# Second parts of split weights issued right behind the first parts in a two-layer streaming encoder

## The chip, the cores and the metric

The kernel runs on one core of a Trainium2 chip. The metric is the device time of one execution in microseconds (us). The kernel before took 1279.29 us, the median of three runs (1280.31, 1279.29 and 1275.89).

The core's engines each work through their own instructions in the order in which the program lists them, and wait for each other by semaphores: PE (TensorE) multiplies matrices, with its weight loads shown as PEld; DVE (VectorE) and ACT (ScalarE) work elementwise; POOL (GpSimd) does little here; SP (SyncE) issues the DMA transfers.

## The reference

A trunk of two layers over 256 frames with 1024 channels, in float32. Each layer has a token mixer and a channel mixer, both modulated by a conditioning vector (shift, scale, gate):

```python
# token mixer: an RG-LRU group (512 channels) beside differential attention (4 heads)
h  = rmsnorm(x) * (1 + scale) + shift
z  = h @ w_in                      # 1024 x 2560: lru input, gelu gate, q, k, v
a  = exp(-8 * sigmoid(conv(z) @ wa + ba) * softplus(-lam))
y0 = scan(a, sqrt(1 - a*a) * (i * conv(z))) * gelu(z_gate)
y1 = rmsnorm((softmax(q0 k0) - lambda * softmax(q1 k1)) @ v)   # rope on q, k; chunk mask
x  = x + gate * (concat(y0, y1) @ w_out)
# channel mixer: layer 0 dense, layer 1 top 2 of 8 experts
x  = x + gate * ((silu(h @ wg) * (h @ wu)) @ wd)               # inner width 3072
```

The weights are some 420 MB of float32, read once from HBM.

## The kernel before

**Splitting.** Every product is to be as exact as float32, and is built from three matmuls over numbers of a shorter format: with w = wh + wl and x = xh + xl it sums xh·wh, xh·wl and xl·wh (`mm3`, L203 to L213; in the token mixer's input projection the same three are written out: `proj_T`, L568 to L583, and `queries_keys`, L585 to L597, where L593 holds the two products with wh and L596 the one with wl). For the activations `cut` makes the parts (`hh`, L565, and `hl`, L566). Weights arrive by DMA as `raw` tiles of 128 x 2048 (10 buffers) and are split in pieces of 128 x 1024 by `split_next` (L137): ACT copies the piece into the short format, the first part `wh` (L147); DVE subtracts it from the raw piece, the second part `wl` (L148). Both have 4 buffers. Not all weights are split: those of the modulation (`adaps`, L404) and of most expert units are multiplied as they are.

**The order.** It is written by hand: each engine runs its instructions as the Python code records them. The unit of this order is the quarter chunk, one piece of weights. `quarter` (L159) first runs the `tick`: all elementwise or small PE work that was put off to this quarter by `after` (constants at the start, rotary embedding, softmax, the gates and the scan of the LRU, silu, and so on). Then `refill` (L169) splits pieces until 4 are ready, and `piece` (L164) hands one of them to the matmuls. The second part of a piece is not recorded with the first: `split_next(False)` puts it as a function into `self.rests`, and `split_rest` (L154) records the oldest one:

```python
nc.scalar.activation(wh, raw, AF.Copy)                                               # L147
self.rests.append(lambda: nc.vector.tensor_tensor(wl, raw, wh.bitcast(F32), op=ALU.subtract))  # L148
self.ready.append((wh, wl))
if whole:
    self.split_rest()
```

`refill` counts the second parts that were pending when it began (`old`), splits the first parts of new pieces, and then records `old` second parts. So the wl of a piece is recorded one `refill` after its wh, with the tick between them standing ahead of it in DVE's order; `piece` makes up for it when the piece that it hands out would still lack its wl.

**The stages, by the trace.** Layer 0: token mixer to about 155 us, dense SwiGLU to 365 us. Layer 1: token mixer 370 to 485 us, routing to 508 us, then eight expert units (`glu_unit`, three of them on all 256 frames, with split weights: from 508, 690 and 790 us; the others partly or wholly on unsplit weights). In the mixers, `adaps`, `hps` (L541), `colps` (L415) and the gain (L417) make the modulated input of one quarter of the channels, and `zps` are queries and keys; `vps` are the values and `wops` the output projection (L208 to L210). In a big expert unit `mul` (L858, DVE) multiplies silu by the up projection and `flip` (L863, PE) transposes the result two quarters later.

Of the kernel before, what the change touches and what calls it, by code (L numbers as in the profile page):

```python
# [74 lines left out]
class Kernel:  # L75
# [86 lines left out]
        return self.piece(n)  # L162

    def piece(self, n):  # L164
        if len(self.rests) >= len(self.ready):
            self.split_rest()
        return [w.rearrange("p (a b) -> p a b", a=n) for w in self.ready.pop(0)]

    def refill(self, most=1 + AHEAD):  # L169

        old = len(self.rests)
        while len(self.ready) < most and self.spos < self.limit and self.split_at(self.spos * PIECE // RAW):
            self.split_next(False)
        for _ in range(old):
            self.split_rest()

    def warm(self, n):

# [1746 lines left out]
```

## Time and profile before

| | before |
|---|---|
| median of 3 runs | 1279.29 us (1275.89 to 1280.31) |
| profiled execution, its span | 1276.7 us, 1274.8 us |
| PE busy | 1223.6 us, 96% |
| DVE busy | 687.7 us, 54%; wl (L148) 344 times, 408.2 us |
| ACT busy | 554.2 us, 43%; wh (L147) 344 times, 359.7 us |
| mean granted TensorE clock | 0.986 of 2.4 GHz |

The profile is of one execution. A row of its timeline gives start and duration in us, engine, line, operation, output<-input, and in brackets how long the engine had been idle before and what ended the idle time. Busy shares are averages over stages: an engine that is 96% busy over the whole can still wait at a few places, and those places are what a change of order can reach.

### The profile page before, as it was taken

To read this page: it belongs to the slowest core of one execution; us is meant where nothing else is said; L and a number is where in the kernel's file an instruction comes from. 1 tells how busy PE (TensorE), PEld (TensorE's weight loads), DVE (VectorE), ACT (ScalarE), POOL (GpSimd) and SP (SyncE) were. 2 spreads that over 40 slices of the span, in tenths; PEclk is the share of its full clock that TensorE was granted. 3 is DMA by queue.
4 is the path that set the end of the run, shared out by engine and by line. 5 is a ranking of instruction groups with operands and counts; after the bars stand their busy time and mean duration, and the time that the engine had idled before them with its cause. 6 is when DMAs were issued, how large, how long until landed. Compare 5 with 4: busy or idle time off the path is not lost.

```text
span 1274.8 us, 19410 instructions
## 1 busy us (share of the span) xinstructions
PE 1223.6 (96%) x7702; PEld 813.0 (64%) x7702; DVE 687.7 (54%) x992; ACT 554.2 (43%) x809; POOL 21.3 (2%) x40
## 2 busy tenths in 40 slices
PE   5899999999999989999998999999999999999995
PEld 4777799999978768788434888888433333333332
DVE  4677687776567766988404889999401001100102
ACT  3466454444444945888203888788210000010001
POOL 1000100000000000000000000000000000000001
PEclk9999999999999988999999999999999999999998
DMA  9976788887544346899999999999999999998994
GB/s 374 418 304 229 275 315 300 308 298 293 191 183 168 131 171 256 300 338 343 364 418 419 419 418 419 391 363 366 343 419 418 418 419 417 364 375 348 418 418 194
DMA packets 63427, 424.68 MB, mean 333 GB/s; under 512 B 7734, under 2 KB 7990, under 8 KB 15072
## 3 DMA queue, kind: packets, MB, share of 16 engines
q1 hardware_dynamic: 63072, 423.28, 84.5%
q8 instruction: 62, 1.02, 0.3%
q14 instruction: 37, 0.30, 0.1%
q0 software_dynamic: 256, 0.09, 0.0%
HBM read 422.29 MB, written 1.05 MB: 332 GB/s over the span
## 4 chain that ended last, share of the span: by engine, by line
PE 81%; DMA 7%; DVE 6%; ACT 4%; issue 1%; SPq 0%; POOL 0%; POOLq 0%; DVEq 0%; ACTq 0%
PE gps L889 4%; PE ups L889 4%; PE gps L580 4%; PE gps L582 4%; PE gps L578 4%; PE gps L942 3%; PE yps L981 3%; PE ups L942 3%; PE bps L954 3%; DMA raw<-i_md 3%; DMA raw<-i_mu 3%; PE ups L209 2%; PE yps L209 2%; PE ups L208 2%; PE yps L210 2%; PE ups L210 2%
## 5 line engine op out<-in xcount | busy, mean ns | idle before, releaser
L148 DVE TENSOR_TENSOR wl<-raw,wh 128x1024 fp32r<-128x1024 f32 x344 | 408.2, 1220 | 57.6 <-ACT wh L147 55.3
L147 ACT ACTIVATE wh<-raw 128x1024 fp32r<-128x1024 f32 x344 | 359.7, 1060 | 168.0 <-PE gps L580 55.9
L580 PE MATMUL gps<-hl,wh 128*128 128x256 f32 x384 | 96.5, 284 | 0.7 <-DVE hl L566 0.7
L578 PE MATMUL gps<-hh,wh 128*128 128x256 f32 x384 | 96.7, 284 | 0.1
L580 PEld LDWEIGHTS gps<-hl,wh 128*128 128x128 f32 x384 | 72.8, 190 | 1.3 <-DVE hl L566 1.1
L578 PEld LDWEIGHTS gps<-hh,wh 128*128 128x128 f32 x384 | 72.8, 190 | 0.5 <-DVE hh L565 0.3
L900 DVE TENSOR_TENSOR sgs<-sgs,ups 128x512 f32<-128x512 f32 x9 | 6.2, 688 | 120.6 <-PE ups L889 120.6
L911 PE MATMUL yps<-raw,hTs 128*64 128x512 f32 x288 | 66.9, 596 | 2.3 <-DMA raw<-i_md 2.1
L947 DVE TENSOR_TENSOR sgm<-sgm,ups 128x512 f32<-128x512 f32 x6 | 4.1, 688 | 116.6 <-PE ups L942 116.6
L889 PE MATMUL ups<-raw,ef 128*64 128x512 f32 x288 | 65.3, 594 | 0.8 <-DMA raw<-i_mu 0.8
L889 PE MATMUL gps<-raw,ef 128*64 128x512 f32 x288 | 66.0, 598 | 0.0
L582 PE MATMUL gps<-hh,wl 128*128 128x256 f32 x384 | 61.7, 283 | 0.0
L209 PE MATMUL gps<-wl,eh 128*128 128x512 f32 x144 | 57.0, 396 | 1.5 <-DVE wl L148 1.5
L208 PE MATMUL gps<-wh,eh 128*128 128x512 f32 x144 | 57.0, 396 | 1.2 <-ACT wh L147 1.2
L208 PE MATMUL yps<-wh,fh 128*128 128x512 f32 x144 | 58.0, 402 | 0.0
L209 PE MATMUL ups<-wl,eh 128*128 128x512 f32 x144 | 56.9, 395 | 0.5 <-DVE wl L148 0.5
L209 PE MATMUL yps<-wl,fh 128*128 128x512 f32 x144 | 56.7, 394 | 0.4 <-DVE wl L148 0.3
L208 PE MATMUL ups<-wh,eh 128*128 128x512 f32 x144 | 56.9, 395 | 0.0
L210 PE MATMUL gps<-wh,el 128*128 128x512 f32 x144 | 56.4, 391 | 0.0
L210 PE MATMUL yps<-wh,fl 128*128 128x512 f32 x144 | 56.3, 391 | 0.0
L210 PE MATMUL ups<-wh,el 128*128 128x512 f32 x144 | 56.3, 391 | 0.0
L582 PEld LDWEIGHTS gps<-hh,wl 128*128 128x128 f32 x384 | 52.8, 190 | 0.0
(329 smaller groups left out, 2038.8 us busy)
## 6 DMA issues: line engine op xcount, KB each, us to landing
raw<-i_mu SPq DMA_DIRECT2D x92, 1024.0 KB, 10.5
raw<-i_md SPq DMA_DIRECT2D x88, 1024.0 KB, 11.8
raw<-i_mg SPq DMA_DIRECT2D x84, 1024.0 KB, 9.5
raw<-i_ada SPq DMA_DIRECT2D x48, 1024.0 KB, 7.5
raw<-i_win SPq DMA_DIRECT2D x20, 1024.0 KB, 9.2
raw<-i_fg SPq DMA_DIRECT2D x12, 1024.0 KB, 6.8
raw<-i_fu SPq DMA_DIRECT2D x12, 1024.0 KB, 6.9
raw<-i_fd SPq DMA_DIRECT2D x12, 1024.0 KB, 6.5
```

The source lines that it names most:

```text
L147: nc.scalar.activation(wh, raw, AF.Copy)
L148: self.rests.append(lambda: nc.vector.tensor_tensor(wl, raw, wh.bitcast(F32), op=ALU.subtract))
L208: mm(out, lhsT=xh, rhs=wh, start=start, stop=False)
L209: mm(out, lhsT=xh, rhs=wl, start=False, stop=False)
L210: mm(out, lhsT=xl, rhs=wh, start=False, stop=stop)
L578: self.nc.tensor.matmul(out, lhsT=w, rhs=hh[:, k, :], stop=False, start=k == 0 and (len(ks) == NK or m + j == 0))
L580: self.nc.tensor.matmul(out, lhsT=w, rhs=hl[:, k, :], start=False, stop=False)
L582: self.nc.tensor.matmul(out, lhsT=wl[:, j * len(ks) + i, :], rhs=hh[:, k, :], start=False, stop=k == NK - 1 and (len(ks) == NK or m + j == 1))
L889: nc.tensor.matmul(ps[c * HALF:(c + 1) * HALF, :], lhsT=eh[:, k, :], rhs=w[c][i // 2][:, i % 2, :], start=k == 0, stop=k == NK - 1)
L911: self.nc.tensor.matmul(y[n * HALF:(n + 1) * HALF, :], lhsT=hT[:, b, c * HALF:(c + 1) * HALF], rhs=w[n][b // 2][:, b % 2, :], start=i == 0 ...
L942: nc.tensor.matmul(ps[q(2 * c + s), :], lhsT=eh[:, k, q(s)], rhs=ws[w][c][i // 2][:, i % 2, :], start=k == 0, stop=k == NK - 1)
L954: nc.tensor.matmul(bp[q(2 * w + c), :], lhsT=eh[:, k, q(2)], rhs=ws[w][c][i // 2][:, i % 2, :], start=k == 0, stop=k == NK - 1)
```

## The change

`refill` records the second part of every piece directly behind its first part, and no longer carries any over; `piece` no longer needs to force one.

```diff
     def piece(self, n):
-        if len(self.rests) >= len(self.ready):
-            self.split_rest()
         return [w.rearrange("p (a b) -> p a b", a=n) for w in self.ready.pop(0)]
 
     def refill(self, most=1 + AHEAD):
-
-        old = len(self.rests)
         while len(self.ready) < most and self.spos < self.limit and self.split_at(self.spos * PIECE // RAW):
-            self.split_next(False)
-        for _ in range(old):
-            self.split_rest()
+            self.split_next()
```

Instructions are neither added nor removed. The orders of PE, ACT, POOL and SP stay as they were, each DMA issue among them. On DVE the wl rows move ahead of the ticks: of some 916 other DVE rows 382 have one wl more ahead of them than before, 28 at the start have two more, and 506 have as many as before. The new file is six lines shorter, so that a line behind L175 has a number lower by 6 there.

DVE at the start of layer 0, where the constants of the rotary embedding are computed (`set_91`); before:

```order
L566 TENSOR_TENSOR hl<-hf,hh 128x256
L260 CAST set_91<-set_91 128x2
L262 TENSOR_SCALAR set_91<-set_91 128x32 x2
...
L276 TENSOR_SCALAR set_91<-set_91 128x64
L277 TENSOR_SCALAR set_91<-set_91 128x64
L148 TENSOR_TENSOR wl<-raw,wh 128x1024 x2
L408 TENSOR_TENSOR row_130<-adaps,row_130 128x128
```

and now:

```order
L560 TENSOR_TENSOR hl<-hf,hh 128x256
L148 TENSOR_TENSOR wl<-raw,wh 128x1024 x2
L254 CAST set_91<-set_91 128x2
L256 TENSOR_SCALAR set_91<-set_91 128x32 x2
...
L270 TENSOR_SCALAR set_91<-set_91 128x64
L271 TENSOR_SCALAR set_91<-set_91 128x64
L402 TENSOR_TENSOR row_130<-adaps,row_130 128x128
```

Two wl, of pieces 2 and 3 (counted from 0), moved from behind the 18 instructions of sine and cosine to ahead of them. Some 20 rows further on the wl of pieces 4 and 5 moved in the same way ahead of the differential attention's lambda (L292 to L309).

DVE in layer 0 ahead of the output projection (`gate0`: the scan's output, cut into hh and hl); the tile numbers tell which piece a wl belongs to. Before:

```order
L763 RECIPROCAL rsum_1081<-sums_1059 128x2
L148 TENSOR_TENSOR wl_1065<-raw_1015,wh_1064 128x1024
L710 TENSOR_TENSOR gate1_914<-gate1_914,th_982 128x1024
L712 SCALAR_TENSOR_TENSOR gate0_865<-a0_983,gate1_914 128x256 x4
L726 TENSOR_TENSOR gate0_865<-gate0_865,gy_1116 128x512
L565 CAST hh_1132<-gate0_865 128x512
```

and now:

```order
L757 RECIPROCAL rsum_1082<-sums_1060 128x2
L148 TENSOR_TENSOR wl_1096<-raw_1093,wh_1095 128x1024
L704 TENSOR_TENSOR gate1_915<-gate1_915,th_983 128x1024
L706 SCALAR_TENSOR_TENSOR gate0_866<-a0_984,gate1_915 128x256 x4
L720 TENSOR_TENSOR gate0_866<-gate0_866,gy_1117 128x512
L559 CAST hh_1133<-gate0_866 128x512
```

The rows read alike, but the wl is that of the next piece (its number 1096 where 1065 stood): at every place from here to the mixer's end one more wl has already been recorded. In layer 1 it is the same.

DVE at the head of the first big expert unit, where the experts are sorted by load (L1401 on); before:

```order
L566 TENSOR_TENSOR el_4875<-ef_4915,eh_4874 128x256
L148 TENSOR_TENSOR wl_4840<-raw_4834,wh_4839 128x1024
L565 CAST eh_4874<-ef_4930 128x256
L566 TENSOR_TENSOR el_4875<-ef_4930,eh_4874 128x256
L1360 TENSOR_TENSOR tops_4964<-tope_4859 128x2
...
L148 TENSOR_TENSOR wl_4994<-raw_4980,wh_4993 128x1024
L148 TENSOR_TENSOR wl_5006<-raw_5003,wh_5005 128x1024
L1401 COPY sort0_5026<-all_5038 128x8
```

and now:

```order
L560 TENSOR_TENSOR el_4875<-ef_4915,eh_4874 128x256
L148 TENSOR_TENSOR wl_4840<-raw_4834,wh_4839 128x1024
L559 CAST eh_4874<-ef_4930 128x256
L560 TENSOR_TENSOR el_4875<-ef_4930,eh_4874 128x256
L148 TENSOR_TENSOR wl_4955<-raw_4952,wh_4954 128x1024
L1354 TENSOR_TENSOR tops_4965<-tope_4859 128x2
...
L148 TENSOR_TENSOR wl_5007<-raw_5004,wh_5006 128x1024
L148 TENSOR_TENSOR wl_5018<-raw_5004,wh_5017 128x1024
L1395 COPY sort0_5027<-all_5039 128x8
```

One wl moved ahead of the gates (L1360, now L1354), so that the wl of one further piece (wl_5018) stands ahead of the sorting.

## Rows read from the trace of the kernel before

**Rows 1.** The page: busy us, share of the span and instructions of each engine.

```profile
PE 1223.6 (96%) x7702; PEld 813.0 (64%) x7702; DVE 687.7 (54%) x992; ACT 554.2 (43%) x809; POOL 21.3 (2%) x40
```

**Rows 2.** Waits of PE: line, releaser, us in total, times, longest.

```profile
PE zps L596 <- DVE wl L148: 7.5, 3, 3.0
PE wops L209 <- DVE wl L148: 5.1, 2, 2.7
PE vps L209 <- DVE wl L148: 2.5, 1, 2.5
```

**Rows 3.** Groups by line: count, busy, mean ns of one, idle before them.

```profile
L148 DVE TENSOR_TENSOR wl<-raw,wh 128x1024 fp32r<-128x1024 f32 x344 | 408.2, 1220 | 57.6 <-ACT wh L147 55.3
```

**Rows 4.** PE's timeline at the start of layer 0.

```profile
19.86 1.95 PE L404 MATMUL adaps<-raw,csil 128*32 128x128 f32 x64
...
24.40 1.07 PE L596 MATMUL zps<-wl,hh 128*128 128x512 f32 x4
...
30.27 2.07 PE L596 MATMUL zps<-wl,hh 128*128 128x512 f32 x4 [2.99 <-DVE wl L148]
32.27 2.50 PE L404 MATMUL adaps<-raw,csil 128*32 128x128 f32 x64
...
42.77 1.36 PE L596 MATMUL zps<-wl,hh 128*128 128x512 f32 x4 [2.50 <-DVE wl L148]
44.06 3.41 PE L404 MATMUL adaps<-raw,csil 128*32 128x128 f32 x64
```

**Rows 5.** DVE's timeline there.

```profile
24.93 0.16 DVE L260 CAST set<-set 128x2 f32<-128x2 int32 x1
...
28.99 2.36 DVE L148 TENSOR_TENSOR wl<-raw,wh 128x1024 fp32r<-128x1024 f32 x2
```

**Rows 6.** PE's timeline, layer 0, output projection.

```profile
115.64 0.80 PE L209 MATMUL wops<-wl,hh 128*128 128x512 f32 x1 [2.36 <-DVE wl L148]
...
118.79 0.40 PE L210 MATMUL wops<-wh,hl 128*128 128x512 f32 x1
...
119.72 1.95 PE L780 MATMUL ops<-v,pTs 128*128 128x128 f32 x16
```

**Rows 7.** DVE's timeline ahead of it.

```profile
107.53 1.23 DVE L710 TENSOR_TENSOR gate<-gate,th 128x1024 f32<-128x1024 f32 x1 [0.84 <-ACT th L709]
```

**Rows 8.** DVE's timeline, layer 1, softmax and gates.

```profile
427.10 0.42 DVE L745 CUSTOM_DVE_ANT_0 sm<-sps,mask 128x256 f32<-128x256 f32 x1 [3.48 <-PE sps L739]
...
431.56 1.23 DVE L702 SCALAR_TENSOR_TENSOR th<-a,th 128x1024 f32<-128x1024 f32 x1 [1.86 <-ACT a L699]
```

**Rows 9.** ACT's timeline, the wh that the moved wl needs.

```profile
427.29 1.04 ACT L147 ACTIVATE wh<-raw 128x1024 fp32r<-128x1024 f32 x1
```

**Rows 10.** PE's timeline, layer 1, output projection.

```profile
447.96 0.50 PE L208 MATMUL wops<-wh,hh 128*128 128x512 f32 x1 [1.30 <-DVE hh L565]
451.19 0.79 PE L209 MATMUL wops<-wl,hh 128*128 128x512 f32 x1 [2.73 <-DVE wl L148]
```

**Rows 11.** DVE's timeline, head of the first big expert unit.

```profile
511.86 5.76 DVE L148 TENSOR_TENSOR wl<-raw,wh 128x1024 fp32r<-128x1024 f32 x5
517.67 0.17 DVE L1401 COPY sort<-all 128x8 f32<-128x8 f32 x1
...
534.00 0.68 DVE L858 TENSOR_TENSOR sg<-sg,ups 128x512 f32<-128x512 f32 x1
```

**Rows 12.** ACT's timeline there.

```profile
517.50 2.94 ACT L147 ACTIVATE wh<-raw 128x1024 fp32r<-128x1024 f32 x3
```

**Rows 13.** PE's timeline there, the flip behind that mul.

```profile
534.90 0.60 PE L863 MATMUL hT<-cst,sg 128*128 128x128 f32 x4
```

**Rows 14.** DVE's timeline, one mul of the second big unit.

```profile
715.95 0.69 DVE L858 TENSOR_TENSOR sg<-sg,ups 128x512 f32<-128x512 f32 x1 [0.28 <-PE ups L210]
```

**Rows 15.** PE's timeline, its flip.

```profile
718.50 0.60 PE L863 MATMUL hT<-cst,sg 128*128 128x128 f32 x4
```

**Rows 16.** Big units: us, busy (count) PE, PEld, DVE, ACT, POOL, clock, DMA, GB/s.

```profile
700.00:900.00 200.00, 200.00 (x914) 164.16 (x913) 183.30 (x183) 160.22 (x180) 0.00 (x0) 1.00 0.99 395
```

## The prediction

> **What bounds the kernel now.** I read the busy times first. PE works 1223.6 us of a span of 1274.8 us [rows 1], so no reordering on another engine can give more than the 51 us in which PE stands. The list of PE's waits comes next: the reader is to look for the lines whose releaser is DVE's wl. Three lines carry 15.1 us in six waits: 7.5 us at the start of layer 0, 5.1 us at the two output projections and 2.5 us at the values of layer 1 [rows 2]. These are what an earlier wl can reach. Then the timelines of the engines at those six places, to see what DVE does ahead of the wl, and at the expert units, where a wl that comes earlier stands in front of something else. The dense SwiGLU and the mid and half expert units have no wait for wl worth counting in that list, and I put them at nothing.
>
> The sum is made against the profiled execution, 1276.7 us; the median of the runs, 1279.29 us, lies 2.6 us above it, and I add that at the end.
>
> **What moves.** The 344 wl take as long as before, 1220 ns each [rows 3]. Whatever is gained or lost is a change in what stands ahead of what on DVE. No DMA is issued by the moved rows. A raw buffer is given back a little earlier at most, so loads are not late by this.
>
> *Start of layer 0.* PE waits 2.99 us at 30.27 and 2.50 us at 42.77 for wl, and behind each wait it works slowly: the four matmuls take 2.07 and 1.36 us where the same four took 1.07, and the 64 of `adaps` 2.50 and 3.41 us where they took 1.95 [rows 4]. That is 1.00 + 0.29 + 0.55 + 1.46 = 3.3 us of clock. Before the first wait DVE runs sine and cosine from 24.93 until the two wl at 28.99 [rows 5], 4.1 us. Now the two wl run first, from 24.93 to 27.3; the first is ready at 26.1, ahead of PE, which comes to it at 30.27 - 2.99 = 27.3. That wait goes. In the second place the wl goes ahead of the lambda rows; it then waits for its wh only, which I price at 0.3 us. The third wait of this line, 7.5 - 2.99 - 2.50 = 2.0 us, stays: the decay constants (L312, L313) still stand ahead of that wl.
>
> New waits: sine and cosine now run from 27.3 to 31.4. PE, not held, ends the 64 `adaps` at about 27.3 + 0.9 + 1.95 = 30.1, and the DVE addition behind them (L408) must wait for 31.4: 1.3 us that PE passes on. The lambda rows, pushed back by two wl (2.4 us), push the next such addition by about 0.65. Sum: -2.99 - 2.50 - 3.3 + 0.3 + 1.3 + 0.65 = -6.5 us. Bounds: -3.2 if the clock gives nothing back, -8.8 if there is no new wait.
>
> The Trainium skill ("TensorE: Matmul & The Clock Gate", Part 1, What's actually happening) says that the slow clock is the default and that activity releases it; this trace agrees in direction, slow rows standing behind the two long waits. By that rule waits of 1.3 us could cost some clock again, which is inside my bounds.
>
> *Output projection of layer 0.* PE waits 2.36 us at 115.64, and the eight matmuls from there to 118.79 take 3.15 us, where four from 118.79 to 119.72 take 0.93 [rows 6]: 3.15 - 1.86 = 1.3 us of clock. The wl in question now stands ahead of L710, so this wait goes. The price is that L710 starts later, by the length of a wl less the 0.84 us for which DVE idled ahead of it waiting for ACT [rows 7]: 1.22 - 0.84 = 0.4 us. hh and hl of both halves are late by that, and PE, which comes 3.7 us earlier, meets them: 0.3 us at the first half, about 0.9 us at the second. Net -2.36 - 1.3 + 1.2 = -2.4 us; bounds -1.0 (no clock) and -3.7 (no new wait).
>
> *Layer 1, values and output projection.* The wait of 2.5 us at the values goes, but PE only runs into the hh of the output projection, which sets the place: at 447.96 it waits for hh, at 451.19 for a wl [rows 10]. The second of these waits goes, since that wl now stands ahead of L710. hh gets later: ahead of the softmax row at 427.10 [rows 8] stands one wl more, whose wh ACT makes only from 427.29 to 428.33 [rows 9]; the wl ends at 429.5, and the row starts 2.4 us late. DVE idles 1.86 us before L702 [rows 8] and takes that much back; 0.55 goes through the gates and the scan to hh. So PE starts at 447.96 + 0.55 = 448.5, and the wl matmul follows at about 448.8 instead of 451.19: -2.4 us. PE still stands some 4 us ahead of hh, so I give back no clock here. Bounds: -0.5 (the 2.4 us of delay reach hh whole) and -5 (hh not late, clock regained).
>
> *Head of the big expert units.* Here the change costs. Ahead of the expert sorting DVE does five wl from 511.86, then sorts from 517.67 [rows 11]. Now the fifth is of the next piece, whose wh is the first of the three that ACT starts at 517.50, behind silu [rows 12]: done at 518.55, wl at 519.7, sorting 2.05 us later. DVE is full from here to the mul at 534.00, which ends at 534.68 [rows 11] and thus at 536.7, while its flip stands at 534.90 on PE [rows 13]: +1.9 us. Bounds: 0 (DVE makes it up on the way) and +3.1 (one wl more).
>
> *All other big units.* mul comes later by one wl, 1.22 us at most. A typical mul ends at 715.95 + 0.69 = 716.64 [rows 14], its flip starts at 718.50 [rows 15]: 1.86 us of slack cover it. At nothing, bounds -1 and +8 (below).
>
> **Sum.** -6.5 - 2.4 - 2.4 + 1.9 = -9.4 us: 1276.7 becomes 1267.3, and with the 2.6 us to the median 1269.9. I predict 1270 us. What PE gains early passes on to the end, because between those places it is PE itself that is full [rows 16]. A case of this kind spans 1264 to 1275.
>
> **The rivals.**
>
> *Slower: DVE held by a wl that waits for its wh.* DVE works in order. A wl recorded right behind its wh in another engine's queue starts when ACT gets there, and everything behind it, mul included, waits as well. Already before, wl waited 55.3 us for wh [rows 3], and in the big units ACT is busy 160 of 200 us and DVE 183 [rows 16]. If a mul comes later not by 1.22 but by 1.22 + 2.05 us (the delay at the head), 3.3 us, it exceeds the slack of 1.86 by 1.4 us; on 17 further units that is +24 us, and with the -9.4 the time is 1279.3 - 9.4 + 24 = 1294 us. The point from which it decides: an average delay of mul of 1.86 + 9.4 / 17 = 2.4 us eats the gain. Against it: only units at whose silu a wl has to wait are hit so, and one wait has to be made up within a unit; DVE has 17 us idle in 200 [rows 16].
>
> The Trainium skill ("TensorE: Matmul & The Clock Gate", Part 1, Architectural detail) calls DVE's queue a strict FIFO with no reordering, which speaks for this rival; the order of the rows in this trace agrees.
>
> *No change: the stream of weights takes it back.* In 700 to 900 the DMA is 0.99 busy at 395 GB/s [rows 16]. If the loads there cannot start earlier although PE comes earlier, PE waits at its first unsplit unit for what it gained: 1276.7 + 1.9 = 1278.6, some 1279 us by the median's scale. Against it: PE waits for no transfer in that stretch, and each load is issued when a buffer comes free, which an earlier PE does.
>
> *Little: waits are refilled and the clock stays down.* The lower ends at the start and at the projections, -3.2 - 1.0 - 0.5, with +1.9: -2.8 us, 1276.5 us.
>
> *More: clock regained and new waits missing.* -8.8 - 3.7 - 5 with 0: -17.5 us, 1262 us.
>
> **Chances.** Forecast 0.67, more gain 0.08, little 0.10, stream 0.06, slower 0.09. What a measurement can tell from no change is 0.3%, 3.8 us: faster is below 1275.5, slower above 1283.1. The forecast and the greater gain, and a quarter of the "little" case, are faster: 0.77. The rest of "little", the stream, and a small part of the slower case that only eats the gain, are the same: 0.15. Slower: 0.08. The range of 8 in 10 leaves out some of the slower case and of the greatest gain, 1263 to 1279.
>
> **What would show it.** Right: PE's waits for wl at L596 fall from three to one, those at the output projections go, the wait for hh in layer 1 grows to about 4 us, and PE's flips show one new wait for mul of about 2 us at the head of the first big unit, none later. Wrong: new waits at later flips (the slower rival), slow clock behind the new waits at L408's consumers, or waits for raw where none were. If the three early terms come out and the end does not, the stream took them.

## The result and the profile after

The changed kernel takes 1264.39 us, the median of four runs (1261.72 to 1266.18), against 1278.34 us before on the same chips: a ratio of 0.989, 95% interval 0.9864 to 0.9917, so 14 us faster. The forecast was 1270 us, 9.4 us faster, in a range of 1263 to 1279. The profiled execution's span is 1260.0 us, where before it was 1274.8. It is the fastest of the four (1261.72 us), 2.7 us below their median, as the one before lies 2.6 us below its own.

PE's list of waits, as in [rows 2] (lines behind L175 are lower by 6):

```profile
PE pT L762 <- ACT pTs L765: 2.7, 1, 2.7
...
PE zps L590 <- DVE wl L148: 2.1, 1, 2.1
...
PE hT L857 <- DVE sg L852: 1.4, 1, 1.4
...
PE wops L202 <- DVE hh L559: 1.3, 2, 0.8
...
PE gps L203 <- DVE wl L148: 1.0, 1, 1.0
...
PE colps L409 <- DVE row L402: 1.0, 1, 1.0
```

Of the 15.1 us in [rows 2] one wait of 2.1 us is left. New are waits of 2.7 us for ACT's copy `pTs`, 1.4 us for a mul and 1.0 us for a row of the modulation.

Since PE runs the same instructions in the same order, the same row can be looked up in both timelines, and the difference of its two starts says how far ahead the changed kernel is there. The last two columns give what a stretch adds to or takes from PE's time, in us; minus is faster:

| PE row | before, us | after, us | ahead by | predicted for this stretch | measured |
|---|---|---|---|---|---|
| hps L541, fourth quarter | 47.39 | 39.78 | 7.6 | -6.5 | -7.6 |
| wops L208, second half, layer 0 | 121.86 | 111.30 | 10.6 | -2.4 | -3.0 |
| pT L768 behind layer 1's first projection | 458.14 | 444.96 | 13.2 | -2.4 | -2.6 |
| warm L182 at the router | 497.81 | 482.91 | 14.9 | nothing | -1.7 |
| hT L863, first late flip | 534.90 | 521.64 | 13.3 | +1.9 | +1.6 |
| gps L209 in the first big unit | 596.14 | 581.56 | 14.6 | nothing | -1.3 |
| ups L889 in the last half unit | 1236.69 | 1221.72 | 15.0 | nothing | -0.4 |

The stretches add up to -15.0 us, where the forecast had -9.4. Behind the row of layer 0's projection PE gives back another 0.3 us there, so by stages the two projections are worth 2.7 and 2.9 us.

Start of layer 0 on PE, the answer to [rows 4]:

```profile
27.05 1.07 PE L590 MATMUL zps<-wl,hh 128*128 128x512 f32 x4
28.05 1.95 PE L398 MATMUL adaps<-raw,csil 128*32 128x128 f32 x64
31.61 0.39 PE L409 MATMUL colps<-cst,row 128*128 128x4 f32 x2 [1.02 <-DVE row L402]
...
36.77 1.20 PE L590 MATMUL zps<-wl,hh 128*128 128x512 f32 x4
37.90 1.95 PE L398 MATMUL adaps<-raw,csil 128*32 128x128 f32 x64
...
47.42 1.21 PE L590 MATMUL zps<-wl,hh 128*128 128x512 f32 x4 [2.06 <-DVE wl L148]
```

Both long waits are gone, the 64 `adaps` take 1.95 us in both places instead of 2.50 and 3.41, and the third wait stays. The granted clock was 0.50 of full speed (its low level, 1.2 of 2.4 GHz) in 30 to 33 us of the kernel before; in the changed one it is 1.00 from 24 to 69 us.

How far ahead PE is at one row also depends on the execution. The changed kernel was profiled a second time (the run `e6_mul_later` below has the same instructions), and there PE has slow rows ahead of every wl that moved:

```profile
18.76 1.05 PE L587 MATMUL zps<-wh,hl 128*128 128x512 f32 x2
```

In the other two profiles these two matmuls take 0.62 us. By 22 us the slow rows cost 2.2 us, so at the fourth quarter this execution is 5.1 us ahead and not 7.6. From 22 us to there it gains 7.4 us: the gain of the stretch is the same, but a single lead can be off by some 2 us.

DVE at the start, the answer to [rows 5]:

```profile
24.93 2.36 DVE L148 TENSOR_TENSOR wl<-raw,wh 128x1024 fp32r<-128x1024 f32 x2
27.21 0.16 DVE L254 CAST set<-set 128x2 f32<-128x2 int32 x1
...
31.27 0.28 DVE L402 TENSOR_TENSOR row<-adaps,row 128x128 f32<-128x128 f32 x1
```

The two wl run first, sine and cosine behind them, and the addition L402 starts only at 31.27: this is the new wait of 1.02 us.

Output projection of layer 0, the answer to [rows 6] and [rows 7], on PE and on DVE:

```profile
105.61 0.40 PE L203 MATMUL wops<-wl,hh 128*128 128x512 f32 x1
...
111.30 0.50 PE L202 MATMUL wops<-wh,hh 128*128 128x512 f32 x1 [0.46 <-DVE hh L559]
```

```profile
85.22 1.23 DVE L148 TENSOR_TENSOR wl<-raw,wh 128x1024 fp32r<-128x1024 f32 x1 [6.18 <-ACT wh L147]
...
100.39 1.23 DVE L704 TENSOR_TENSOR gate<-gate,th 128x1024 f32<-128x1024 f32 x1 [0.92 <-ACT th L703]
```

The wait for wl is gone and hh of the second half is waited for. DVE still stands 0.92 us ahead of L704; it got late one softmax earlier, at 85.22, behind a wl that waits for its wh.

Layer 1 on DVE and PE, the answer to [rows 8] and [rows 10]:

```profile
418.06 1.23 DVE L148 TENSOR_TENSOR wl<-raw,wh 128x1024 fp32r<-128x1024 f32 x1 [4.75 <-ACT wh L147]
419.20 0.42 DVE L739 CUSTOM_DVE_ANT_0 sm<-sps,mask 128x256 f32<-128x256 f32 x1
```

```profile
436.15 1.11 PE L762 MATMUL pT<-cst,sm 128*128 128x128 f32 x4 [2.69 <-ACT pTs L765]
438.10 0.79 PE L202 MATMUL wops<-wh,hh 128*128 128x512 f32 x1 [0.84 <-DVE hh L559]
438.69 0.63 PE L203 MATMUL wops<-wl,hh 128*128 128x512 f32 x1
```

DVE stands 4.75 us in front of a wl whose wh is not made, with the softmax behind it, as predicted (before it stood 3.48 us in front of the softmax itself [rows 8]). PE is 10.3 us ahead when it comes into this stage, the softmax row 7.9 us (427.10 before, 419.20 now), so it is 2.4 us late by that. PE waits, first for ACT's copy, then for hh. The wl of the projection no longer keeps it. The clock is still low behind these waits (0.63 us a matmul where 0.39 is full speed).

Head of the big expert units on DVE, the answer to [rows 11]:

```profile
503.43 1.23 DVE L148 TENSOR_TENSOR wl<-raw,wh 128x1024 fp32r<-128x1024 f32 x1 [1.25 <-ACT wh L147]
504.58 0.16 DVE L1395 COPY sort<-all 128x8 f32<-128x8 f32 x1
...
520.90 0.68 DVE L852 TENSOR_TENSOR sg<-sg,ups 128x512 f32<-128x512 f32 x1
```

and the flip on PE, the answer to [rows 13]:

```profile
521.64 0.66 PE L857 MATMUL hT<-cst,sg 128*128 128x128 f32 x4 [1.42 <-DVE sg L852]
```

The wl in front of the sorting waits for its wh; the sorting starts 1.8 us later than it would by the 14.9 us that the kernel is ahead (517.67 - 14.9 = 502.77), and mul ends at 521.58, in front of a flip that waits 1.42 us. From the sorting to that mul DVE takes 16.32 us, before it took 16.33: the delay passes on whole. Over the whole program wl waits more for wh than in [rows 3], 80.2 us instead of 55.3, in the groups by line:

```profile
L148 DVE TENSOR_TENSOR wl<-raw,wh 128x1024 fp32r<-128x1024 f32 x344 | 410.6, 1221 | 86.0 <-ACT wh L147 80.2
```

### The profile page after: what moved, and what is told of

The parts are those of the page before. It is cut to its first block, busy times and chain, and to the rows that moved or that the text cites. A ratio compares the mean times of both kernels' runs of the same rounds, so it can differ in the third digit from the quotient of the medians.

```text
span 1260.0 us, 19436 instructions
## 1 busy us (share of the span) xinstructions
PE 1216.4 (97%) x7702; PEld 807.5 (64%) x7702; DVE 689.4 (55%) x992; ACT 552.3 (44%) x809; POOL 21.3 (2%) x40
## 3 DMA queue, kind: packets, MB, share of 16 engines
q8 instruction: 62, 1.02, 0.3%
HBM read 422.29 MB, written 1.05 MB: 336 GB/s over the span
## 4 chain that ended last, share of the span: by engine, by line
PE 80%; DMA 7%; DVE 6%; ACT 4%; issue 2%; POOL 0%; SPq 0%; POOLq 0%; ACTq 0%; DVEq 0%
PE gps L883 4%; PE gps L574 4%; PE gps L576 4%; PE gps L572 4%; PE yps L975 3%; PE gps L936 3%; PE ups L936 3%; PE ups L883 3%; PE bps L948 3%; DMA raw<-i_md 3%; DMA raw<-i_mu 3%; PE yps L202 3%; PE yps L203 3%; PE yps L204 3%; PE gps L203 3%; PE gps L202 2%
## 5 line engine op out<-in xcount | busy, mean ns | idle before, releaser
L148 DVE TENSOR_TENSOR wl<-raw,wh 128x1024 fp32r<-128x1024 f32 x344 | 410.6, 1221 | 86.0 <-ACT wh L147 80.2
```

## The experiments

Ratios are to the kernel before, run on the same chip beside them, with their 95% interval.

**Is the gain the sum of its places?** Four kernels record a stretch of the pieces late as before and the rest early. The edit is one condition in the `refill` of the kernel before, which keeps the carrying over (cut short here):

```diff
         old = len(self.rests)
         while len(self.ready) < most and ...:
-            self.split_next(False)
+            self.split_next(not (self.spos < 8))
         for _ in range(old):
             self.split_rest()
```

Only the start late:

> The changed kernel, but the second parts of the first eight pieces (the start of layer 0) are recorded late, as before; everything else as changed. If the gain is the sum of its places, it loses what the start gained in the profiles, 7.6 us: some 7 us faster than before, 1271 us, with waits of 3.0 and 2.5 us for wl back at L596 and the slow adaps rows (2.5 and 3.4 us) with them. Rival, that an early gain is swallowed downstream by the stream of weights: it stays at 14 us faster.

1268.39 us, ratio 0.9937 (0.9914 to 0.9960): 8 us faster than before. In PE's timeline the waits at the start are back, and with them the slow rows:

```profile
30.42 2.03 PE L595 MATMUL zps<-wl,hh 128*128 128x512 f32 x4 [2.95 <-DVE wl L148]
32.38 2.67 PE L403 MATMUL adaps<-raw,csil 128*32 128x128 f32 x64
...
43.06 1.21 PE L595 MATMUL zps<-wl,hh 128*128 128x512 f32 x4 [2.51 <-DVE wl L148]
44.20 3.57 PE L403 MATMUL adaps<-raw,csil 128*32 128x128 f32 x64
```

Only the start early (`self.spos >= 8`):

> The opposite: only the first eight pieces are recorded early, everything else late as before. Sum of places: 7.6 us faster than before, 1271 us, with all waits behind 60 us as before. Rival, that the places are not additive or that the start's gain is given back later: under 3 us faster.

1272.08 us, ratio 0.9952 (0.9933 to 0.9972): 6 us faster by the ratio (the interval is 3.6 to 8.6; the two medians differ by 4.6). The two parts, 8 and 6 us, make the 14 of the whole, each known to some 2.5 us. PE's timeline is closer: this kernel is 4.3 us ahead at layer 0's projection and 4.4 in the last half unit, so nothing is swallowed behind the start. At the fourth quarter it was 6.1 us ahead; the 1.6 us went in slow rows at 51 to 54 us, behind the third wait, where the changed kernel has none (granted clock 0.55 and 1.00). In PE's list all later waits are there as before:

```profile
PE wops L208 <- DVE wl L148: 5.1, 2, 2.7
PE vps L208 <- DVE wl L148: 2.5, 1, 2.5
```

The rest of the mixers late (`8 <= self.spos < 28 or 100 <= self.spos < 128`):

> The changed kernel with the rest of both token mixers late as before (pieces 8 to 27 and 100 to 127). Sum of places: it loses 2.95 us at the output projection of layer 0 and 2.9 us in layer 1, so 8 us faster than before, 1270 us. If the 1.7 us that the profile after gained at the router (its 32 matmuls took 3.6 us where they took 5.4) belongs to the mixers' order, 6.5 us faster; if that is the phase of the clock and not the order, the router's row shows either length whatever this kernel does.

1270.44 us, ratio 0.9949 (0.9927 to 0.9972): 6.5 us faster, so the mixers' order is worth some 7.5 us, more than the 3.0 and 2.6 of the table. The rest is at the router, whose 32 matmuls took 5.35 us before, 3.64 us in all nine profiles in which layer 1's wl are early, and 5.1 us here.

The expert units late (`self.spos >= 128`):

> The changed kernel with the expert units late as before (pieces from 128 on). My prediction's term for the head of the big units, a loss of 1.9 us, says that this kernel is 1.9 us faster than the changed one, 1262.5 us. The profile after says less: the flip's wait of 1.4 us is new, but waits for wl of 0.5, 0.3 and 0.4 us are gone, so 0 to 0.5 us faster than the changed one. If early wl cost more in the other big units than shows there (slower rival), it is over 3 us faster.

1264.47 us, ratio 0.9902 (0.9879 to 0.9925): no different from the changed kernel within the intervals. On PE this kernel loses 0.9 us from the router to the last half unit (12.85 us ahead, then 11.93), the changed one none (14.9, then 15.0). Early wl cost nothing in the expert units on balance that these runs could tell: by the timelines the flip's wait is paid by waits for wl that are gone.

**Are the slow rows at the start the clock?** The kernel before with idle matmuls on PE in the two waits:

```diff
+        if self.spos < 12:
+            self.warm({2: 22, 4: 18}.get(k, 0))
         for t, ts in enumerate(tiles):
             for i in range(2):
                 mm(z[i][t], lhsT=hh[:, k, ts], rhs=wl[:, i, :], ...)
```

> The kernel before, with 22 and 18 idle matmuls (ones times ones) put on PE in the two long waits for wl at the start of layer 0; the order on DVE is untouched, so the waits as such stay. If the 3.3 us of slow rows behind them are the clock falling because PE stands, those rows go back to full speed (the 64 adaps from 2.5 and 3.4 us to 1.95) and PE is 3.3 us earlier at 60 us, with no second part earlier. If the rows are slow because of what else runs there (the DMA at full rate), or because the filling only replaces the wait, nothing changes, or it is later by what the filling overruns.

PE's timeline, the fillings and what stands behind them:

```profile
27.02 5.08 PE L182 MATMUL warm<-ones 128*128 128x128 f32 x44
31.85 1.18 PE L598 MATMUL zps<-wl,hh 128*128 128x512 f32 x4
32.95 1.95 PE L404 MATMUL adaps<-raw,csil 128*32 128x128 f32 x64
...
40.22 4.18 PE L182 MATMUL warm<-ones 128*128 128x128 f32 x36
44.16 1.18 PE L598 MATMUL zps<-wl,hh 128*128 128x512 f32 x4
45.26 1.95 PE L404 MATMUL adaps<-raw,csil 128*32 128x128 f32 x64
```

The rows are at full speed with no wl earlier and the DMA as busy as before (1.01 to 1.04 in 30 to 33 and 42 to 48 us, granted clock 1.00): it is the clock, and it does not fall where PE is kept busy. The filling was too long and made PE 1.7 and 1.3 us later (each of its matmuls is two in the trace), and the two speed-ups took back 1.47 and 1.62 us, 3.1 together where 3.3 was expected. So the time stays: 1277.38 us, ratio 0.9999 (0.9985 to 1.0012).

**How near is the slower rival?** In the big units the slack between mul and flip went from 1.86 us typically ([rows 14, 15]) to 1.01, as between this mul on DVE and its flip on PE in the profile after:

```profile
702.05 0.68 DVE L852 TENSOR_TENSOR sg<-sg,ups 128x512 f32<-128x512 f32 x1
```

```profile
703.74 0.60 PE L857 MATMUL hT<-cst,sg 128*128 128x128 f32 x4
```

Two operations more ahead of every mul:

```diff
+                for _ in range(2):
+                    nc.vector.scalar_tensor_tensor(sg[t], sg[t], 1.0, sg[t], op0=ALU.mult, op1=ALU.max)
                 nc.vector.tensor_tensor(sg[t], sg[t], up[t], op=ALU.mult)
```

> The changed kernel with two more operations on DVE ahead of each of the 18 mul of the big expert units (sg = max(sg, sg), 0.7 us each, the output is the same), 1.4 us. In the profile after, the slack from the end of mul to its flip is 0.06 to 1.95 us, 1.01 typically (before 1.86). If the slack is what keeps the slower rival away, PE waits at the flips for the sum of what exceeds it, some 8 us (4 to 12), and the time rises by that. If early wl cost nothing in the big units for another reason (PE has room of its own), it rises by less than 2 us.

As first written the added lines applied to units of two tiles only, which the big units are not, so its instructions are the changed kernel's: 1264.31 us, a repeat of it, with the same wait of 1.4 us at the flip. With the lines in force:

> The changed kernel with two more operations on DVE ahead of each of the 18 mul of the big expert units (sg = max(sg, sg), the output is the same), now on the units' one tile of tokens; the run before asked for two tiles, which these units do not have, so it added nothing. As there: if the slack of 0.06 to 1.95 us ahead of the flips, 1.01 typically, is what keeps the slower rival away, 1.3 us more per mul makes PE wait some 8 us (4 to 12) at the flips. If early wl are harmless in the big units for another reason, under 2 us.

In PE's list of waits:

```profile
PE hT L859 <- DVE sg L854: 12.2, 14, 2.9
```

1282.83 us, ratio 1.0033 (1.0014 to 1.0053): 18 us more than the changed kernel and slower than the kernel before. PE waits at 14 of 18 flips, 12.2 us where I expected 8 (4 to 12). The rest is not in this line. By the timelines of the two kernels some 3 us of it are slow rows (0.63 us for 0.39 behind the first late flip, 0.79 and 0.62 at 691 us), 1.1 us new waits for wl, and the remainder pieces of some 0.2 us behind the flips. So the rival is real, and the changed kernel typically stands one microsecond per mul away from it (0.06 to 1.95 us).

**Can the start's last waits go?** The constants in other places: the cosine half behind the wl of pieces 4 and 5, the decay constants a tick later.

```diff
-        for i in range(2):
+        def half(i):
...
+        half(0)
         yield
...
+        half(1)
         self.nlam = const.tile([P, L], F32, name="nlam")
...
-"setup": [3, 4, 5, 5, 6, 11]
+"setup": [3, 4, 5, 5, 7, 11]
```

> The changed kernel with the constants of the start put where DVE is idle: the cosine half of the rotary constants goes from ahead of the second adaps addition to behind the wl of pieces 4 and 5, and the decay constants (eight pairs) from tick 6 to tick 7, behind the wl of piece 6. If the waits left in the profile after are only DVE's order, the 1.02 us at colps and the 2.06 us at L590 go, 3 to 3.5 us less than the changed kernel with the clock behind the second. Rival: the constants are needed where they stood, and the waits come back at the rotary embedding or the gates: no change.

1264.61 us, ratio 0.9896 (0.9882 to 0.9910), no gain. The two waits that were aimed at are gone, and PE's timeline shows two others:

```profile
42.88 0.39 PE L412 MATMUL colps<-cst,row 128*128 128x4 f32 x2 [2.47 <-DVE row L405]
56.67 0.63 PE L648 MATMUL qkT<-cst,rot 128*128 128x128 f32 x4 [2.27 <-DVE rot L642]
```

A second try: sine at tick 1, where DVE idles, cosine at 3, decay at 10 and 11 (`"setup": [1, 3, 4, 5, 5, 10, 11]`, a `yield` between the halves):

> The changed kernel with the constants of the start on other ticks: the sine half of the rotary constants at tick 1, in the 2.6 us in which DVE is idle ahead of the second addition; the cosine half stays at tick 3; the decay constants at tick 10 and 11, behind the rotary embedding. The earlier try put them where DVE turned out to be full (new waits of 2.5 us at colps and 2.3 us at qkT). If DVE's order is the whole reason for the waits left in the start, the 1.02 us at colps and the 2.06 us at L590 go and nothing takes their place by 100 us: 3 us less in the profile, 1261 us. If DVE is full over the whole start, they come back at the rotary embedding or the softmax: under 1 us.

The new wait in PE's timeline:

```profile
58.66 0.63 PE L649 MATMUL qkT<-cst,rot 128*128 128x128 f32 x4 [2.06 <-DVE rot L643]
```

1262.97 us, ratio 0.9874 (0.9834 to 0.9915). From 22 us on PE gains 3.4 us on the changed kernel until 47 us, and loses it all in front of the rotated keys and with the clock behind that wait. DVE is not full over the whole start: here it is busy 6.3 of 10 us from 24 us, 7.8 from 34 and 9.8 from 44. It is full from 44 us on, and there both tries leave the decay constants ahead of the rotary rows that PE waits for (in the second, which was to have them behind, 3.1 us from 53.30). The wait of 2.47 us at colps in the first try came from the cosine half, put in front of an addition, and from 1.05 us in which DVE waits for ACT. So twice a wait that went came back at about its length; constants placed behind all rotary rows were not tried. This is the lowest median of all, but 1.4 us under the changed kernel is less than these intervals tell apart.

**What makes mul late at the head?** On top of the first placing, the wl that waits for its wh in front of the sorting is recorded late (`self.split_next(self.spos != 137)`, in the `refill` that carries over).

> The kernel of the run before this one, with one wl alone recorded late as before: that of the tenth piece of the expert units, which stands ahead of the sorting and waits for its wh there. If my reading of the head of the big units is right, that one wait is what makes mul late: PE's wait of 1.4 us at the first late flip falls to 0.2 to 0.4 us, 1 to 1.4 us less in the profile. Rival, that mul is late because DVE is simply one wl fuller: the wait stays at 1 us or more.

In PE's list of waits:

```profile
PE hT L864 <- DVE sg L859: 1.2, 1, 1.2
```

1263.51 us, ratio 0.9897 (0.9877 to 0.9918). The wait falls from 1.4 to 1.2 us only: the wait for the wh is worth 0.2 us of it. Counted from the router's row, the sorting does come 1.8 us earlier than in the kernel of the first placing, but the held wl now stands behind it and still ahead of mul (1.14 us), and another wl there waits 0.32 us for its wh. In the next kernel the last wl ahead of that mul is recorded behind it, on the changed kernel (`self.spos != 146`):

> The changed kernel, but one wl (piece 146, the last one recorded ahead of the late mul at the head of the big units) is recorded behind that mul, as before. The wait of 1.4 us at its flip stood at 1.2 us when the wl that waits for its wh was held back, so I now take the plain length of one wl more on a full DVE as the cause: PE's wait falls to 0.3 us or less, 1.2 us less in the profile. If it is the wh after all (ACT paces DVE here, whatever the order), the wait stays above 0.8 us.

The flip in PE's timeline:

```profile
523.24 0.66 PE L860 MATMUL hT<-cst,sg 128*128 128x128 f32 x4 [0.28 <-DVE sg L855]
```

The wait is 0.28 us, 1.14 less: mul is late by the length of one wl on a DVE that is full. 1263.72 us, ratio 0.9883 (0.9843 to 0.9923), not told apart from the changed kernel; a wait for wl of 0.24 us comes back behind the flip.

**The router's clock.** The kernel before, with idle matmuls in layer 1's three waits (in `mm3` and `piece`):

```diff
+        self.warm({120: 5}.get(at, 0))
+        self.fill = {117: 11, 120: 12}.get(at, 0)
...
             mm(out, lhsT=xh, rhs=wh, start=start, stop=False)
+            n, self.fill = self.fill, 0
+            self.warm(n)
```

> The kernel before, with idle matmuls (11, 5 and 12) on PE in its three waits of layer 1: for wl at the values, for hh and for wl at the output projection; the order on DVE stays that of before. In all profiles so far the router's 32 matmuls took 5.1 to 5.4 us where layer 1's wl were late, and 3.64 us where they were early. If that is the clock's history (PE stands and the clock falls at the projection, and the next fall comes at another place), they take 3.64 us here too, and the projection's matmuls go back to full speed. If it is something else in the order, they stay at 5.1 to 5.4 us.

The router's matmuls in PE's timeline, here and, below, in the kernel before:

```profile
494.62 3.64 PE L1328 MATMUL lps<-rout,hf 128*128 128x8 f32 x32
```

```profile
492.61 5.35 PE L1323 MATMUL lps<-rout,hf 128*128 128x8 f32 x32
```

3.64 us with the order of before, so it is the clock's history and not DVE's order as such. The low clock is not gone, it comes later. Windows of the kernel before and, below, of the changed one, with busy us (count) of PE, PEld, DVE, ACT and POOL, then granted clock, DMA share and GB/s:

```profile
495.00:500.00 5.00, 5.00 (x24) 5.00 (x25) 3.03 (x9) 3.39 (x4) 0.00 (x0) 0.50 1.00 421
```

```profile
480.00:485.00 5.00, 4.58 (x38) 4.39 (x37) 4.24 (x14) 5.00 (x7) 0.00 (x0) 0.89 1.00 423
485.00:490.00 5.00, 5.00 (x25) 5.00 (x25) 3.16 (x10) 1.01 (x3) 0.00 (x0) 0.50 0.99 372
```

Before, the router's matmuls run from 492.61 to 497.96, most of that time at the low level; in the changed kernel they end at 483.06, and the low level begins behind them. Added up from the granted clock in stretches of 4 us, the clock is low for some 10 us there in the kernel before and some 7 us in the changed one and in this run. The filling was again too long (4.6 us late at the projection, 0.3 us late behind the router; 0.7 us of this comes from ahead of the fillings), and the time is unchanged: 1277.24 us, ratio 0.9994 (0.9978 to 1.0009).

## Why the prediction was right, and where it was off

**Start.** Right in place and size: -7.6 for -6.5 us. The two waits and the clock went as worked out (the clock term shown by the filling), the third wait stayed, and the new wait at colps was 1.02 us for 1.3; behind it the rows stay at full speed. What was too much is the price at the lambda rows, 0.3 + 0.65 us; those waits did not come.

**Output projection, layer 0.** Right in size, -3.0 for -2.4, and in the waits: hh of the second half cost 0.46 us where I had 0.9, the 0.3 at the first half did not come, and 0.3 more went behind the second. The clock term was read from eight slow matmuls; the trace has seven, which makes it 1.5 us and not 1.3. That hh is late by 0.4 us (0.36 in the trace) came out by luck: I let DVE take back the 0.84 us that it stood ahead of L710, and it stands there 0.92 us now. The delay is made at the softmax before, where DVE waited for PE's scores and now waits for a wh.

**Layer 1.** Right in size, -2.6 for -2.4, and in the reason: PE runs into what DVE makes late by waiting for a wh. The softmax row is 2.4 us late as said, the 1.86 us of idle time ahead of L702 are taken back whole, and hh is 0.5 us late for 0.55. Which wait takes the place of the one at the values was not right: I had some 4 us ahead of hh; it is 2.69 us for ACT's copy of the transposed softmax and 0.84 us for hh.

**Left out: the router.** "Nothing" between layer 1's projection and the expert units was wrong by 1.7 us. I looked for waits, and there is none: the same 32 matmuls ran at another clock. The filling shows that what PE does 40 us earlier decides when the clock falls there. How is open: in the changed kernel the projection runs at a low clock too (0.63 us a matmul at 438.69), and the router is fast.

**Head of the big units.** Size right, 1.6 for 1.9 us, cause wrong. I put all of the delay on a wl that waits for its wh in front of the sorting. The sorting was late by 1.8 us as said and the delay did pass on whole, but the flip's wait of 1.42 us falls only to 1.23 with that wait taken away, and to 0.28 with one wl fewer ahead of mul. So the term that failed is the wait for the wh: it is worth 0.2 us, and the length of one wl more ahead of mul 1.14 us. That the size came out is partly luck. I also counted no gain there: waits of PE for wl of 0.48 us (at 513.13 in the kernel before), 0.27 (at 537.78) and 0.42 (at 596.14) went. The first lies ahead of the flip and is in the 1.6; the other two, with the rows that run faster there, paid 1.3 us back.

**The other big units.** Right: no new waits, slack typically 1.01 us left. The point from which the slower rival decides was set at 2.4 us of delay; at 0.85 + 1.3 = 2.15 us the kernel was already slower than before. The added operations also load a DVE that was busy 183 of 200 us [rows 16], so this is the price of delay and load together, and a bare delay was not tried.

**The stream of weights** swallowed nothing that the runs could tell: PE's lead of 14.9 us at the router is 15.0 us in the last half unit. The price of this rival was put on the profiled execution's scale; on the median's it is 1281 us and not 1279.

So the sum, -9.4 us, fell short of the -15.0 of the two profiles by the router (1.7), the gain in the expert units (1.7), the start (1.1), the projections (0.8) and the head (0.3). None of this is of the other sign, so nothing made up for anything else. The median of 1264.39 us lies inside the range of 1263 to 1279, near its lower end.

## What to carry to other kernels

When an instruction is moved forward in an engine that works in order, list for each place what it now stands in front of and how long that thing may be late; the moved one costs its whole length there, and also its own wait. A wait that is removed on the matrix engine is worth its length and the slow clock behind it where there is one, which the rows show as the same work at two durations: behind the waits of 2.99, 2.50, 2.36 and 2.73 us the rows were slow, behind that of 2.04 us at 54.96 in the kernel before they were not. And if taking one wait away brings another of the same length from the same engine, look up whether that engine is full over the stretch, or whether the moved work only stands ahead of the next thing that is waited for.

## What was not expected

The clock in one stage depended on the waits of a stage some 40 us earlier: the router's 32 matmuls took 3.64 us in all nine profiles with early wl in layer 1 and in the one with the waits filled, and 5.1 to 5.4 us in the four others. At the start of layer 0 the clock also differs between two executions of the same instructions, by 2.2 us of PE's time. And 1.3 us more per mul cost 18 us over 18 mul, of which PE's waits at the flips show 12.2.
